# A diffusion block in float32 on one core: the later modulation sums go from VectorE to ScalarE and adding transfers

## The chip, the cores and the metric

The kernel runs on one core of a Trainium2 chip. The metric is the device time of one execution in microseconds (us). TensorE multiplies matrices, VectorE and ScalarE work element by element, GpSimd clears tiles and issues some transfers, SyncE issues the large ones. In the profile they are PE (with PEld for the loading of its weights), DVE, ACT, POOL and SP; a q behind the name (SPq) means the engine's instruction queue.

## What is computed

One layer of a diffusion backbone on 256 latent tokens and 256 context tokens of width 2048. Six modulation vectors come from the conditioning vector and one large matrix, `ada_w` (2048 x 12288):

```python
mod_lat = (silu_c @ ada_w[l] + ada_b[l])[:, None, :]
sh1, sc1, g1, sh2, sc2, g2 = jnp.split(mod_lat, 6, axis=-1)
h = modulate(rms_norm(x, norm1_w[l]), sh1, sc1)
f, q, k, v, z, gate = split_proj(h @ w_in[l])
att = neighborhood_attention(q, k, v, k_ctx, v_ctx, na_rpb[l])
x = x + g1 * gated_merge(f, att, z, gate, *mix_w)
h2 = modulate(rms_norm(x, norm2_w[l]), sh2, sc2)
x = x + g2 * conv_ffn(h2, *ffn_w)
return rms_norm(x, final_norm_w)
```

The shift and scale of the first norm (`sh1`, `sc1`) are needed at once. The other four vectors, `g1`, `sh2`, `sc2` and `g2`, are the later modulation: 4 x 2048 columns, in 16 blocks of 512 columns, each a sum over the 2048 channels.

## The kernel before

All weights stream from HBM in the order of their use. `chunk` (L84) cuts them from blocks of 3072 columns on 128 partitions (1.5 MB); SyncE loads each block with one transfer (L89) into one of three buffers `raw` (two more exist until the keys and values are done). A chunk is 1024 columns (512 KB), so a block holds three.

A chunk of ordinary weights is split for TensorE: ScalarE casts it to a high part `whi` (L98), VectorE subtracts to get the low part `wlo` (L99), and three products of the parts follow (L108 to L110). There are three buffers for such split chunks.

The later modulation runs beside this. A job is one block of 512 columns and takes eight chunks; the class `Side` (L188) traces one such piece after every few ordinary chunks, by a rate: 0.5 in the last groups of keys and values, 1 in the queries, 0.65 from the attention to the output projection, 0.2 in the gated MLP. So the chunks of later modulation lie between the others in the same blocks. `ada_sum` (L214) sums a piece: the channels lie on partitions, and VectorE multiplies each half chunk (512 columns) by a column of `sc` and adds it to an accumulator, in one instruction (L219). What is left is a sum over the partitions, by TensorE with ones: `ada_col` (L237) for `sh2` and `sc2`, with the accumulator `acc`, and `ada_row` (L223) for `g1` and `g2`, where the accumulator is the gate's own tile `g`, cleared by GpSimd and with its bias row loaded.

The order on each engine is set by a scheduler when the program is built, and each engine works through its own in order, waiting on semaphores. GpSimd's queue also holds the loads of small inputs and of the attention's biases (L428, two buffers). Stages in the profile: norm 1, keys and values to 252 us; queries to 300; attention, Fourier mixing and spatial gating, then gates and branch projections, to some 860; output projection and norm 2 to 985; the gated MLP after that.

Of the kernel before, what the change touches and what calls it, by code (L numbers as in the profile page):

```python
# [8 lines left out]
F32 = mybir.dt.float32  # L9
# [6 lines left out]
P = 128  # L16
# [38 lines left out]
def block_kernel(ctx: ExitStack, tc: tile.TileContext, a: dict):  # L55
    nc = tc.nc
    act, dve, pe = nc.scalar, nc.vector, nc.tensor

# [1 line left out]
    const = ctx.enter_context(tc.tile_pool(name="const", bufs=1))  # L60
    rawp = ctx.enter_context(tc.tile_pool(name="rawp", bufs=RAW_BUFS))
    spl = ctx.enter_context(tc.tile_pool(name="spl", bufs=3))
    tmp = ctx.enter_context(tc.tile_pool(name="tmp", bufs=T2K))
    small = ctx.enter_context(tc.tile_pool(name="small", bufs=4))
    pp = {}

    def psum_phase(name, **bufs):
        """banks of the accumulators, of the attention and of everything else"""
        if pp:
            pp["stack"].close()  # L70
        pp["stack"] = ExitStack()
        pp["pool"] = pp["stack"].enter_context(tc.tile_pool(name="ps_" + name, bufs=1, space=PSUM, reuse_waits="tile"))
        pp["bufs"] = bufs
# [6 lines left out]

    # the weights stream in, in the order of their use: blocks of RAWN columns, one transfer each
    stream = a["stream"]
# [28 lines left out]

# [1 line left out]
    ident = const.tile([P, P], F32, name="ident")  # L113
# [18 lines left out]

    # conditioning vectors: silu, split for the tensor engine, filled up to the columns of an array tile
    sc = const.tile([P, KT, 2], F32, name="sc")
    act.activation(sc, cc, AF.Silu)

# [1 line left out]
    rb_pool = ctx.enter_context(tc.tile_pool(name="rb", bufs=KT, side="left"))  # L138
    # the inputs wait where the low parts of the normed ones will be
    xs = [rb_pool.tile([P, 512], F32, name="xs", tag="rb") for _ in range(KT)]  # L140
# [3 lines left out]
    h_hi = ra_pool.tile([P, KT, 512], F32R, name="h_hi")  # L144
    # latent tokens in columns 0..255, context tokens and later the branch results in 256..511
    b_hi = h_hi[:, :, T:2 * T]
# [4 lines left out]

# [1 line left out]
    x_stack = ExitStack()  # L153
# [5 lines left out]
    act.copy(cs4[:, :, 0:2], sc)  # L159
    # brings in the table that the norm needs  # L160
    warm = small.tile([P, 1], F32, name="warm", tag="warm", bufs=1)
# [22 lines left out]

# [1 line left out]
    # sums over the contraction tiles on VectorE, a piece after every few chunks  # L186
    class Side:
        """Work that is traced piece by piece among the weights, `rate` pieces for each chunk of them."""  # L188

# [23 lines left out]

    def ada_sum(acc, blk):  # L214
        for c in range(8):
            w = chunk(1024, "ada_l", blk, c)
            for kk in range(2):
                k = c * 2 + kk
                dve.scalar_tensor_tensor(acc, w[:, kk * 512:(kk + 1) * 512], sc[:, k, 0:1], acc,  # L219
                                         op0=ALU.mult, op1=ALU.add)  # L220
            yield

    def ada_row(dst, blk, brow):  # L223
        """dst = the 512 columns of the block, on every partition."""
        acc = dst()
        nc.gpsimd.memset(acc, 0.0)
        nc.gpsimd.dma_start(acc[0:1], a["adab_rows"][brow])
        yield from ada_sum(acc, blk)
        hi, lo = split_w(acc, 512)
        o = psum("misc")  # L230
        pe.matmul(o, ones_r, hi[:, 0:512], start=True, stop=False)
        pe.matmul(o, ones_r, lo[:, 0:512], start=False, stop=True)
        act.copy(acc, o)
# [3 lines left out]
    def ada_col(which, blk, b):  # L237
        acc = tmp.tile([P, 512], F32, name="acc", tag="acc", bufs=2)
        nc.gpsimd.memset(acc, 0.0)
        yield from ada_sum(acc, blk)  # L240
        o = psum("misc")
        for j in range(4):
            pe.matmul(o[:, j:j + 1], acc[:, j * P:(j + 1) * P], ones[:, 0:1], start=True, stop=True)  # L243
        dst = mod2[:, which, 4 * b:4 * b + 4]
        dve.tensor_tensor(dst, o[:, 0:4], adab[:, 2 + which, 4 * b:4 * b + 4, 0], op=ALU.add)
        if which == 1:
            dve.scalar_tensor_tensor(dst, dst, 1.0, nw[:, 1, 4 * b:4 * b + 4, 0], op0=ALU.add, op1=ALU.mult)
# [8 lines left out]

# [1 line left out]
    def ada_part(k, c, pm):  # L258
        """products with the few conditioning rows, on four column tiles of the array side by side"""
        src = chunk(1024, "ada_e", k, c)  # L260
        for q in range(4):
            pe.matmul(pm[32 * q:32 * q + 32, 0:2 * P], cs4[:, 4 * c + q, :], src[:, 2 * q * P:2 * (q + 1) * P],  # L262
                      start=(c == 0), stop=(c == KT // 4 - 1))
# [21 lines left out]
    def kv_part(g, task, i, n):  # L285
        """a piece of a task: 512 columns of keys or values for n channels of group g"""
        k0, ng = KV_GROUPS[g]
# [44 lines left out]

    # the modulation of a group's channels is spread among the pieces of the group before, LEAD parts ahead
    for g, (k0, n) in enumerate(KV_GROUPS):
# [9 lines left out]

# [1 line left out]
    convs = load_const("convs", [P, FT, 4])  # L346
# [34 lines left out]
    def proj_a(key, nk, lhs, ntt, evac):  # L381
        """lhs(k, t): the split stationary operand of contraction tile k, token tile t; 512 columns of weights move."""
        outs = [psum() for _ in range(ntt)]
# [21 lines left out]

# [1 line left out]
    # branch results, transposed: f in 0..3, attention in 4..11, gMLP in 12..15  # L407
    # the queries of a head wait where its result will be
    for b in range(4):
# [51 lines left out]

# [1 line left out]
    f_sb = [None, None]  # L463
# [16 lines left out]

# [1 line left out]
    u = [None, None]  # L482
# [38 lines left out]

# [1 line left out]
    g1_stack = ExitStack()  # L523
# [7 lines left out]
    for nb in range(NB):  # L531
        gate = {}
        for br in range(3):
            def ev_g(t, o, br=br, nb=nb):
                gate[br, t] = t2k()
                act.activation(gate[br, t], o, AF.Sigmoid)
                if nb == NB - 1 and br == 2 and t == 1:
                    # brings in the table that the next norm needs
                    warm = small.tile([P, 1], F32, name="warm", tag="warm", bufs=1)
# [16 lines left out]

# [1 line left out]
    fp = ctx.enter_context(tc.tile_pool(name="fp", bufs=1, side="right", reuse_waits="tile"))  # L558
# [12 lines left out]
    def ev_o(t, o, c0, c1, part):  # L571
        cs = slice(c0, c1)
        # the gates of these columns are there
        assert len(later_mod.jobs) <= NB - 1 - c0 // 512, len(later_mod.jobs)
# [5 lines left out]
    for nb in range(NB - 1):  # L580
        proj_a(("wo", nb), KT, lhs_m, NT, lambda t, o, nb=nb: ev_o(t, o, nb * 512, (nb + 1) * 512, nb))
    # the last columns in two parts; of the second one token tile after the other
    woh = m_stack.enter_context(tc.tile_pool(name="woh", bufs=KT // 4, side="left", reuse_waits="tile"))
# [15 lines left out]

# [1 line left out]
    banks = [psum(tag) for tag in ("acc", "acc", "misc", "misc", "att", "att")]  # L601
# [36 lines left out]

# [1 line left out]
    g2p = ctx.enter_context(tc.tile_pool(name="g2p", bufs=1, side="left", reuse_waits="tile"))  # L640
# [43 lines left out]
    def down(c, hid):  # L684
# [35 lines left out]

        # the last columns one token tile after the other, so that the first one's end hides behind the second
        nb = NB - 1
# [41 lines left out]
def _host_layout(inp):  # L764
# [6 lines left out]
    def chan(w, n=KT):  # L771
        """[n*P] -> [P, n]"""
        return w.reshape(n, P).T

    def kblk(w):
        """[K*P, n] -> [P, K*n]"""
        K = w.shape[0] // P
# [20 lines left out]
    A["fnw"] = np.broadcast_to(g["final_norm_w"], (P, D))  # L798
    # transforms of the two Fourier axes (shapes alone)
    n = np.arange(T)  # L800
# [5 lines left out]
    A["dft_h"] = np.stack([np.cos(ah), -np.sin(ah)], axis=1) * float(P) ** -0.5  # L806
    # relative position bias laid out by query and key, the constant fill outside the window
    rpb = g["na_rpb"][0]
# [12 lines left out]
def _host_stream(inp, stream):  # L821
    """The weights in the order of their use: one contiguous run for each partition of each block."""
    import numpy as np
# [62 lines left out]
```

## Time and profile before

| | us |
|---|---|
| median of 2 runs | 1638.84 |
| the runs | 1638.11, 1639.57 |
| span of the profiled execution | 1640.9 |
| TensorE busy | 1605.3 |
| VectorE busy | 1096.6 |
| ScalarE busy | 742.0 |

The durations below come from the one profiled execution, whose span is 2.1 us above the median of the runs; the profile gives no other time for that execution. A busy share says how long an engine had an instruction in it. DMA share is the mean busy share of the core's 16 DMA engines. The clock granted to TensorE in a window stands as a fraction of full speed, and is 1.00 in all stages that matter here.

### The profile page before, as it was taken

How to read it: one execution, taken by the hardware profiler on the slowest of the kernel's cores; microseconds unless marked ns; L12 is line 12 of the kernel's file. 1: busy time of each engine (PE TensorE's matmuls, PEld its weight loads, DVE VectorE, ACT ScalarE, POOL GpSimd, SP SyncE). 2: the span in 40 equal slices, each digit the busy share in tenths (PEclk: the TensorE clock that was granted, in tenths of full speed). 3: DMA queues.
4: the chain of work that ended last, by engine and by line, in shares of the span. 5: the costliest groups of instructions: out<-in, count | busy, mean ns of one | idle time of the engine just before them, and what ended most of it. 6: DMA issues, size and time to landing. Idle time of an engine off the chain costs nothing.

```text
span 1640.9 us, 23497 instructions
## 1 busy us (share of the span) xinstructions
PE 1605.3 (98%) x9742; PEld 1383.1 (84%) x9742; DVE 1096.6 (67%) x1471; ACT 742.0 (45%) x986; POOL 28.5 (2%) x60
## 2 busy tenths in 40 slices
PE   5999999999999999999998999999999999999997
PEld 3667789878888888888888999899989998899896
DVE  4755668979987886544566666566666665555757
ACT  6423313557534444434454444444444444344344
POOL 1000001000100000000001000000000000000000
PEclk9999999999999999999999999999999999999999
DMA  9777747746687786544662565666665655454543
GB/s 380 304 308 291 285 149 289 299 170 247 224 318 290 290 305 267 187 181 178 237 226 113 208 224 212 220 225 229 231 222 216 221 227 184 180 183 186 192 180 129
DMA packets 38813, 377.80 MB, mean 230 GB/s; under 512 B 4945, under 2 KB 4961, under 8 KB 8881
## 3 DMA queue, kind: packets, MB, share of 16 engines
q1 hardware_dynamic: 36864, 369.66, 60.0%
q0 software_dynamic: 1840, 6.63, 1.1%
q8 instruction: 76, 1.25, 0.3%
q14 instruction: 33, 0.26, 0.1%
HBM read 374.17 MB, written 2.10 MB: 229 GB/s over the span
## 4 chain that ended last, share of the span: by engine, by line
PE 96%; DMA 2%; DVE 1%; ACT 1%; SPq 0%; issue 0%; ACTq 0%; DVEq 0%
PE ps_acc L108 30%; PE ps_acc L110 30%; PE ps_acc L109 30%; PE ps_misc L262 2%; DMA raw<-in_w 1%; PE ps_att L108 0%; PE ps_misc L271 0%; PE ps_att L109 0%; PE ps_att L110 0%; DMA xs<-in_xct 0%; PE ps_att L445 0%; PE ps_misc L243 0%; DVE t2k L610 0%; SPq L166 0%; DVE wlo L99 0%; PE ps_misc L552 0%
## 5 line engine op out<-in xcount | busy, mean ns | idle before, releaser
L99 DVE TENSOR_TENSOR wlo<-raw,whi 128x1024 fp32r<-128x1024 f32 (+1 forms) x504 | 606.6, 1206 | 358.9 <-ACT whi L98 355.8
L98 ACT CAST whi<-raw 128x1024 fp32r<-128x1024 f32 (+1 forms) x504 | 519.9, 1034 | 597.6 <-PE ps_acc L110 367.0
L109 PE MATMUL ps_acc<-h_lo,whi 128*128 128x256 f32 (+1 forms) x1664 | 482.4, 290 | 0.0
L108 PE MATMUL ps_acc<-h_lo,whi 128*128 128x256 f32 x1408 | 396.2, 281 | 3.7 <-ACT hm L622 3.7
L110 PE MATMUL ps_acc<-h_lo,wlo 128*128 128x256 f32 x1408 | 395.9, 281 | 0.0
L109 PEld LDWEIGHTS ps_acc<-h_lo,whi 128*128 128x128 f32 x1664 | 314.8, 189 | 5.0
L108 PE MATMUL ps_acc<-whi,h_hi 128*128 128x512 f32 x736 | 293.0, 401 | 0.0
L110 PE MATMUL ps_acc<-whi,h_lo 128*128 128x512 f32 x736 | 292.7, 398 | 0.0
L109 PE MATMUL ps_acc<-wlo,h_hi 128*128 128x512 f32 x736 | 290.3, 394 | 0.0
L108 PEld LDWEIGHTS ps_acc<-h_lo,whi 128*128 128x128 f32 x1408 | 266.7, 189 | 4.2 <-ACT hm L622 3.9
L110 PEld LDWEIGHTS ps_acc<-h_lo,wlo 128*128 128x128 f32 x1408 | 266.8, 189 | 0.0
L108 PEld LDWEIGHTS ps_acc<-whi,h_hi 128*128 128x128 f32 x736 | 138.0, 188 | 36.5 <-issue 5.0
L109 PEld LDWEIGHTS ps_acc<-wlo,h_hi 128*128 128x128 f32 x736 | 139.0, 189 | 33.0 <-issue 0.5
L110 PEld LDWEIGHTS ps_acc<-whi,h_lo 128*128 128x128 f32 x736 | 137.8, 187 | 33.6 <-issue 0.5
L108 PE MATMUL ps_acc<-whi,hid_hi 128*128 128x512 f32 (+1 forms) x358 | 140.8, 393 | 0.0
L110 PE MATMUL ps_acc<-whi,hid_lo 128*128 128x512 f32 (+1 forms) x358 | 140.1, 391 | 0.0
L109 PE MATMUL ps_acc<-wlo,hid_hi 128*128 128x512 f32 (+1 forms) x358 | 139.2, 389 | 0.0
L219 DVE SCALAR_TENSOR_TENSOR g<-raw,sc,g 128x512 f32<-128x512 f32 x128 | 95.7, 748 | 26.0 <-DMA raw<-in_w 24.8
L219 DVE SCALAR_TENSOR_TENSOR acc<-raw,sc,acc 128x512 f32<-128x512 f32 x128 | 95.6, 747 | 7.9 <-DMA raw<-in_w 6.3
L108 PE MATMUL ps_acc<-h_hi,whi 128*128 128x512 f32 (+1 forms) x256 | 88.0, 344 | 0.7 <-DVE v L310 0.7
L110 PE MATMUL ps_acc<-h_hi,wlo 128*128 128x512 f32 (+1 forms) x256 | 85.6, 338 | 0.0
L110 PEld LDWEIGHTS ps_acc<-whi,hid_lo 128*128 128x128 f32 x358 | 67.2, 188 | 16.4
(186 smaller groups left out, 1359.5 us busy)
## 6 DMA issues: line engine op xcount, KB each, us to landing
raw<-in_w SPq DMA_DIRECT2D x231, 1536.0 KB, 6.5
xs<-in_xct SPq DMA_DIRECT2D x16, 256.0 KB, 5.6
bias<-in_bias POOLq DMA_DIRECT2D x16, 128.0 KB, 3.8
x<-in_x_tok POOLq DMA_DIRECT2D x1, 2048.0 KB, 8.7
out_dram<-x SPq DMA_DIRECT2D x8, 256.0 KB, 3.1
raw<-in_fnw POOLq DMA_DIRECT2D x1, 1024.0 KB, 5.3
dft_n<-in_dft_n POOLq DMA_DIRECT2D x1, 512.0 KB, 3.8
gnw<-in_gnw POOLq DMA_DIRECT2D x1, 256.0 KB, 4.2
```

Of the source, the lines that this page charges most:

```text
L98: act.copy(hi, src)
L99: dve.tensor_tensor(lo, src, hi.bitcast(F32), op=ALU.subtract)
L108: pe.matmul(out, l_hi, r_hi, start=start, stop=False)
L109: pe.matmul(out, l_hi, r_lo, start=False, stop=False)
L110: pe.matmul(out, l_lo, r_hi, start=False, stop=stop)
L219: dve.scalar_tensor_tensor(acc, w[:, kk * 512:(kk + 1) * 512], sc[:, k, 0:1], acc, op0=ALU.mult, op1=ALU.add)
L262: pe.matmul(pm[32 * q:32 * q + 32, 0:2 * P], cs4[:, 4 * c + q, :], src[:, 2 * q * P:2 * (q + 1) * P], start=(c == 0), stop=(c == KT // 4 - 1))
```

## The change

`ada_sum` no longer uses VectorE for the products. ScalarE multiplies each half chunk by its column, the first chunk of a block into a new tile `part` (1024 columns, two buffers), the seven others in place in the raw buffer. For those seven GpSimd issues a transfer from the raw buffer to `part` that adds as it writes. After the last, VectorE adds the two halves of `part`; `ada_row` adds the result to the gate's tile, `ada_col` uses `part` instead of `acc`, whose clears are gone. The room that GpSimd's transfers have for descriptors is set to 8192.

```diff
+    adap = ctx.enter_context(tc.tile_pool(name="adap", bufs=1))
...
-    def ada_sum(acc, blk):
+    def ada_sum(part, blk):
+
         for c in range(8):
             w = chunk(1024, "ada_l", blk, c)
             for kk in range(2):
-                k = c * 2 + kk
-                dve.scalar_tensor_tensor(acc, w[:, kk * 512:(kk + 1) * 512], sc[:, k, 0:1], acc,
-                                         op0=ALU.mult, op1=ALU.add)
+                ks = slice(kk * 512, (kk + 1) * 512)
+                act.activation((w if c else part)[:, ks], w[:, ks], AF.Copy, scale=sc[:, 2 * c + kk, 0:1])
+            if c:
+                nc.gpsimd.dma_start(part, w, accum_op=ALU.add)
             yield
+        dve.tensor_tensor(part[:, 0:512], part[:, 0:512], part[:, 512:1024], op=ALU.add)
+
+    def ada_part_of():
+        return adap.tile([P, 1024], F32, name="part", tag="part", bufs=2)
...
         acc = dst()
         nc.gpsimd.memset(acc, 0.0)
         nc.gpsimd.dma_start(acc[0:1], a["adab_rows"][brow])
-        yield from ada_sum(acc, blk)
+        part = ada_part_of()
+        yield from ada_sum(part, blk)
+        dve.tensor_tensor(acc, acc, part[:, 0:512], op=ALU.add)
...
-        acc = tmp.tile([P, 512], F32, name="acc", tag="acc", bufs=2)
-        nc.gpsimd.memset(acc, 0.0)
+        acc = ada_part_of()
         yield from ada_sum(acc, blk)
...
-    nc = _bacc.Bacc("TRN2", target_bir_lowering=False, num_devices=1)
+    nc = _bacc.Bacc("TRN2", target_bir_lowering=False, num_devices=1, dynamic_dma_scratch_size=8192)
```

The rest of the diff takes comments out. Lines of the changed kernel lie up to nine further down: L219 becomes L221 (the multiplication) and L223 (the transfer), L98 and L99 become L99 and L100, L89 becomes L90.

The order on the engines, at three places. ScalarE in the first gates and branch projections (window 430 to 640 us of the profile before), a piece of the order before; `raw` with a number is one block of weights, `whi` the high part of a chunk, L536 the gate's activation:

```order
L98 CAST whi_3991<-raw_3989 128x1024
L98 CAST whi_4007<-raw_3989 128x1024
L98 CAST whi_4042<-raw_4040 128x1024
L98 CAST whi_4058<-raw_4040 128x1024
L536 ACTIVATE t2k_4034<-ps_acc_3877 128x512
L536 ACTIVATE t2k_4036<-ps_acc_3878 128x512
L98 CAST whi_4078<-raw_4076 128x1024
L98 CAST whi_4096<-raw_4076 128x1024
```

and about the same place now (the numbers of the tiles are counted anew, L544 is the former L536):

```order
L221 ACTIVATE raw_3942<-raw_3942,sc_92 128x512
L544 ACT_TABLE_LOAD
L544 ACTIVATE t2k_3876<-ps_acc_3713 128x512
L544 ACTIVATE t2k_3878<-ps_acc_3714 128x512
L99 CAST whi_3926<-raw_3901 128x1024
L221 ACTIVATE raw_3967<-raw_3967,sc_92 128x512
L99 CAST whi_3944<-raw_3942 128x1024
L221 ACTIVATE raw_3967<-raw_3967,sc_92 128x512
L99 CAST whi_3963<-raw_3942 128x1024
```

Between the casts stand multiplications in place, some of a block that is loaded after the one cast next; each has to wait for its block's landing, and the casts behind it wait with it. In the order before, such instructions stood on VectorE.

GpSimd in the attention, before, with what each waits for (names with DMASW are landings of its own transfers, with DMAHW those of SyncE's loads):

```order
L428 DMA bias_2544<-in_bias 128x256 [waits DMAHW4_49,DMAHW3_49,DMAHW6_49,DMAHW1_49,DMASW1_49]
L428 DMA bias_2585<-in_bias 128x256 [waits DMASW2_49]
L239 MEMSET acc_2336 128x512 [waits PE_49]
L239 MEMSET acc_2781 128x512 [waits DVE_49,PE_49]
L428 DMA bias_2647<-in_bias 128x256 [waits DMASW3_49,DMASW1_49,DVE_49]
L428 DMA bias_2688<-in_bias 128x256 [waits DMASW4_49,DMASW2_49,DVE_49]
L239 MEMSET acc_3433 128x512 [waits PE_49]
L428 DMA bias_2750<-in_bias 128x256 [waits DMASW5_49,DMASW3_49,DVE_49]
L428 DMA bias_2801<-in_bias 128x256 [waits DMASW6_49,DMASW4_49,DVE_49]
```

and now:

```order
L223 DMA part_2360<-raw_2391 128x1024 [waits DMASW1_49,DMASW0_49,Activation_49]
L223 DMA part_2360<-raw_2457 128x1024 [waits DMASW2_49,DMAHW0_49,DMASW1_49,Activation_49]
L223 DMA part_2360<-raw_2494 128x1024 [waits DMAHW1_49,DMASW2_49,Activation_49]
L223 DMA part_2360<-raw_2494 128x1024 [waits DMASW3_49,Activation_49]
L223 DMA part_2360<-raw_2560 128x1024 [waits DMAHW2_49,DMASW4_49,Activation_49]
L436 DMA bias_2676<-in_bias 128x256 [waits DVE_49]
L223 DMA part_2360<-raw_2664 128x1024 [waits DMASW7_49,DMAHW3_49,DMASW5_49,Activation_49]
L436 DMA bias_2717<-in_bias 128x256 [waits DVE_49]
L223 DMA part_2812<-raw_2879 128x1024 [waits DMAHW5_49,PE_49,Activation_49]
L436 DMA bias_2780<-in_bias 128x256 [waits DMASW6_49,DVE_49]
```

The loads of the biases now stand between adding transfers, and each of these waits for ScalarE and for the landing of the transfer before it or, with a new `part`, for what used that tile last.

SyncE's loads in the first gates, before:

```order
L89 DMA raw_3919<-in_w 128x3072 [waits DMAHW3_49,DVE_49,Activation_49]
L89 DMA raw_3955<-in_w 128x3072 [waits DMAHW4_49,DVE_49,Activation_49]
L89 DMA raw_3989<-in_w 128x3072 [waits DMAHW5_49,DVE_49]
L89 DMA raw_4040<-in_w 128x3072 [waits DMAHW6_49,DVE_49]
L89 DMA raw_4076<-in_w 128x3072 [waits DMAHW7_49,DVE_49]
```

and now:

```order
L90 DMA raw_3901<-in_w 128x3072 [waits DMAHW1_49,DMASW2_49,DVE_49]
L90 DMA raw_3942<-in_w 128x3072 [waits DMAHW2_49,DMASW3_49,DVE_49]
L90 DMA raw_3967<-in_w 128x3072 [waits DMAHW3_49,DMASW7_49,DVE_49]
L90 DMA raw_4004<-in_w 128x3072 [waits DMAHW4_49,DMASW1_49,DVE_49]
L90 DMA raw_4040<-in_w 128x3072 [waits DMAHW5_49,DMASW2_49,DVE_49]
L90 DMA raw_4091<-in_w 128x3072 [waits DMAHW6_49,DMASW3_49,DVE_49]
```

A load now also waits for one of GpSimd's transfers (DMASW), the one that read the buffer's block last.

## Rows read from the trace of the kernel before

**Rows 1.** The page: busy times of the engines, and the chain by engine.

```profile
PE 1605.3 (98%) x9742; PEld 1383.1 (84%) x9742; DVE 1096.6 (67%) x1471; ACT 742.0 (45%) x986; POOL 28.5 (2%) x60
...
PE 96%; DMA 2%; DVE 1%; ACT 1%; SPq 0%; issue 0%; ACTq 0%; DVEq 0%
```

**Rows 2.** Windows: PE, PEld, DVE, ACT, POOL busy (instructions), clock, DMA share, GB/s.

```profile
24.00:92.00 68.00, 66.77 (x435) 44.76 (x427) 42.84 (x81) 30.26 (x54) 0.00 (x0) 1.00 0.84 335
92.00:202.00 110.00, 109.93 (x674) 78.50 (x669) 67.18 (x116) 35.19 (x57) 0.00 (x0) 1.00 0.78 298
...
252.00:300.00 48.00, 47.34 (x398) 46.91 (x397) 40.39 (x52) 18.45 (x22) 1.06 (x2) 1.00 0.81 314
300.00:430.00 130.00, 128.63 (x642) 103.70 (x641) 114.60 (x220) 83.19 (x132) 12.52 (x24) 1.00 0.59 217
430.00:640.00 210.00, 210.00 (x927) 169.97 (x926) 172.86 (x205) 91.81 (x102) 0.49 (x1) 1.00 0.79 300
...
985.00:1600.00 615.00, 615.00 (x4310) 572.75 (x4310) 381.83 (x454) 278.02 (x340) 0.56 (x1) 1.00 0.56 207
```

**Rows 3.** Windows of line L219 alone: VectorE busy (instructions), then as before.

```profile
92.00:202.00 110.00, 14.95 (x20) 1.00 0.78 298
...
252.00:300.00 48.00, 17.97 (x24) 1.00 0.81 314
300.00:430.00 130.00, 27.66 (x38) 1.00 0.59 217
430.00:640.00 210.00, 69.30 (x93) 1.00 0.79 300
...
985.00:1330.00 345.00, 37.43 (x50) 1.00 0.61 224
```

**Rows 4.** Waits of SyncE and of GpSimd: us in total, times, longest.

```profile
SPq L89 <- DVE wlo L99: 1021.8, 157, 33.0
...
POOL bias L428 <- DVE ps_att L431: 99.2, 12, 18.0
```

**Rows 5.** Waits of ScalarE, 430 to 640 us.

```profile
ACT whi L98 <- PE ps_acc L110: 97.8, 61, 2.2
```

**Rows 6.** Timeline of ScalarE, 541 to 549 us: start, duration, instruction, idle before.

```profile
544.47 1.05 ACT L98 CAST whi<-raw 128x1024 fp32r<-128x1024 f32 x1 [1.75 <-PE ps_acc L110]
547.27 1.05 ACT L98 CAST whi<-raw 128x1024 fp32r<-128x1024 f32 x1 [1.75 <-PE ps_acc L110]
```

**Rows 7.** The page: DMA issues, count, KB each, median us to landing.

```profile
raw<-in_w SPq DMA_DIRECT2D x231, 1536.0 KB, 6.5
...
x<-in_x_tok POOLq DMA_DIRECT2D x1, 2048.0 KB, 8.7
...
raw<-in_fnw POOLq DMA_DIRECT2D x1, 1024.0 KB, 5.3
dft_n<-in_dft_n POOLq DMA_DIRECT2D x1, 512.0 KB, 3.8
```

**Rows 8.** Lines by shape: count, busy us, mean ns of one, idle before.

```profile
L219 DVE SCALAR_TENSOR_TENSOR g<-raw,sc,g 128x512 f32<-128x512 f32 x128 | 95.7, 748 | 26.0 <-DMA raw<-in_w 24.8
L219 DVE SCALAR_TENSOR_TENSOR acc<-raw,sc,acc 128x512 f32<-128x512 f32 x128 | 95.6, 747 | 7.9 <-DMA raw<-in_w 6.3
...
L547 DVE TENSOR_TENSOR t2k<-t2k 128x512 f32<-128x512 f32 x16 | 10.4, 683 | 0.0
...
L745 ACT ACTIVATE x<-x,rstd 128x512 f32<-128x512 f32 x4 | 2.7, 711 | 0.2 <-DVE rstd L568 0.2
```

**Rows 9.** DMA issues in 302 to 303 us, and in 319.9 to 320.1 us.

```profile
bias<-in_bias POOLq DMA_DIRECT2D x1, 128.0 KB, 7.0
...
bias<-in_bias POOLq DMA_DIRECT2D x1, 128.0 KB, 2.3
```

## The prediction

> **What bounds the kernel now.** I read the page's busy times and its chain first. TensorE is busy 98% of the 1640.9 us span and holds 96% of the chain that ended last [rows 1]. The idle rest is 1640.9 - 1605.3 = 35.6 us, most of it before the first weights. So whatever is taken off VectorE, no more than 35.6 us can come back, and the sum below looks for what is added.
>
> Second, the windows by stage [rows 2]. The reader is to see that TensorE is full in all of them, while the share of the DMA engines is not: 0.78 at 92 to 202 us, 0.81 at 252 to 300 (queries), 0.59 at 300 to 430 (attention), 0.79 at 430 to 640 (the rest of gating, first gates), 0.56 in the gated MLP. The same window view for the line of the sums alone [rows 3] tells why: the stages with a high share are those in which the modulation weights come in beside the others. A piece is two instructions, so there are 10, 12, 19 and 46.5 pieces in these four stages and 25 in 985 to 1330.
>
> Third, the waits. SyncE stood 1021.8 us in front of its next load until VectorE's last split freed a buffer [rows 4]; with three buffers of 1.5 MB each load starts when one is released, and no sooner. ScalarE waits on TensorE for its split buffers (97.8 us in 430 to 640) [rows 5], so splits run up to three chunks ahead; a chunk is 2.8 us of TensorE, the distance between casts [rows 6]. The lead is thus at most 3 x 2.8 = 8.4 us, and a load takes 6.5 us from issue to landing [rows 7]. Any further delay of a release soon reaches TensorE.
>
> **The change part by part.**
>
> *VectorE.* Removed: 256 instructions of 0.748 us, 95.7 + 95.6 = 191.3 us [rows 8]. Added: 16 joins of halves and 8 sums for the rows, 24 x 0.683 us by an addition of the same shape (L547) = 16.4 us [rows 8]. Net -175 us, beside a TensorE that hardly waits for VectorE: gain 0 to 35.6 us by the idle above; I take 0, since the largest idle parts lie at the start and at the tail, where there is no sum.
>
> *ScalarE.* Added: 256 multiplications. The nearest row is L745, a scaled copy in place by a column of scales, 0.711 us [rows 8]: 182 us in all. By stage: 430 to 640, 91.8 + 93 x 0.711 = 158 of 210 us; 252 to 300, 18.5 + 24 x 0.711 = 35.5 of 48; 300 to 430, 83.2 + 38 x 0.711 = 110 of 130 [rows 2, 3]. There is room in each and the wait on TensorE [rows 5] hides it: 0. If the cover is gone, the cast behind a multiplication is late by the wait of that multiplication for its block, which VectorE's sums had before too (the order of ScalarE in the change section).
>
> *GpSimd's transfers.* Added: 16 blocks x 7 = 112 transfers of 512 KB, in the five stages 7/8 of the pieces: 8.75, 10.5, 16.6, 40.7 and 21.9. Each waits for the multiplication and for the landing of the one before on the same tile, and SyncE's next load waits for it (the orders of GpSimd and SyncE): a release that ended with VectorE now ends with a landing. No row shows an adding transfer. By landing, the nearest rows of the same queue are 512 KB in 3.8 us, 1024 KB in 5.3 us and 2048 KB in 8.7 us [rows 7]; the first is the transfer if adding costs nothing, the last if it takes four times the data. By engine time: 300 GB/s at a share of 0.79 is 380 GB/s when all 16 are busy [rows 2], so 524,288 bytes take 1.38 us per pass. An adding transfer must read the weights and the sum and write the sum: two reads, 1 MB. I take two passes, 2.76 us, the row of 1024 KB; the ends are less than one pass and four passes.
>
> The Trainium skill has a rule on this ("Collectives: The Full Stack", section "The bandwidth ceiling: the fold count and why AG ≠ RS ≠ AR"): an add in the DMA path is slow not by the addition but since it reads two sources, which halves the rate. By that rule it is two passes; no run here shows it yet.
>
> *The sum* is demand against time, in us of the 16 engines:
> - 252 to 300: 0.81 x 48 = 38.9, plus 10.5 x 2.76 = 29.0, is 67.9 in 48.
> - 430 to 640: 0.79 x 210 = 165.9, plus 40.7 x 2.76 = 112.3, is 278.2 in 210.
> - 300 to 430: 0.59 x 130 = 76.7, plus 16.6 x 2.76 = 45.8, is 122.5 in 130.
> - 92 to 202: 0.78 x 110 = 85.8, plus 24.2, is 110.0 in 110; there are five buffers here, I take 0.
> - 985 to 1330: 0.61 x 345 = 210, plus 60, is 270 in 345; a piece comes every 13.8 us, longer than even 8.7 us: 0.
>
> Full use is not to be had with three buffers: the highest share of a stage in this trace is 0.84, at 24 to 92 [rows 2]. Between 0.84 and 1 I take 0.92. Then 67.9 / 0.92 = 73.8 (+25.8), 278.2 / 0.92 = 302.4 (+92.4), 122.5 / 0.92 = 133.2 (+3.2): +121 us. At a share of 1 it is 19.9 + 68.2 = +88; at 0.84, 32.8 + 121.2 + 15.8 = +170. The span becomes 1640.9 + 121 = 1762, and the median of the runs lies 2.1 us below the span: **1760 us**, between 1727 and 1809 for this case alone.
>
> *The rest.* Eight clears on GpSimd go, and an engine busy 2% [rows 1] gains nothing for the path. The smaller descriptor scratch I price at 0; were it too small, GpSimd's issues would grow longer.
>
> **Rivals.**
>
> *One pass (0.22).* Adding costs no more than a copy: 53.4 / 0.92 = 58.0 (+10.0) and 222.1 / 0.92 = 241.4 (+31.4), with nothing at 300 to 430: +41, 1680 us; 1656 at a share of 1, 1709 at 0.84. For it: the 512 KB row is as quick as the others. Against it: the sum must be read as well.
>
> *Not slower (0.10).* The transfers fit into the gaps of the queue. The place is 430 to 640, where the engines stand idle 210 - 165.9 = 44 us; it decides where one transfer takes under 44 / 40.7 = 1.08 us of the engines (252 to 300: 9.1 / 10.5 = 0.87 us), or where loads slide into the emptier 300 to 430. Then VectorE's freed time releases other blocks sooner and the time is 1637 to 1640 us, with a small chance of a few us more gained. Against it: one plain pass is 1.38 us, and three buffers let little slide.
>
> By the Trainium skill ("DMA: Bandwidth & Descriptors", section "Anatomy of one DMA — SWDGE (gpsimd) path") a transfer from GpSimd takes 2 us and its bytes at 436 GB/s, an estimate of 3.2 us for 512 KB; seven in a chain are 22.4 us, less than the 36 us that eight pieces have in 430 to 640, so by it alone the chain keeps up and this rival holds. The trace agrees only where the queue is empty: of two 128 KB transfers one landed in 2.3 us, and one beside loads in 7.0 us [rows 9].
>
> *Three or four passes (0.15).* Adding is slower than its bytes. Four passes, 5.52 us each: (38.9 + 58.0) / 0.92 = 105 (+57), (165.9 + 224.7) / 0.92 = 425 (+215), (76.7 + 91.6) / 0.92 = 183 (+53), and 92 to 202 (85.8 + 48.3) / 0.92 = 146 (+36): +361, some 2000 us. Three passes: +41, +153, +28 and +23, +245, 1884 us. For it: nothing in the trace; against it: nothing either.
>
> *GpSimd's queue (0.08).* The biases of the attention stand in it 99.2 us for their buffers, 12 waits, the longest 18.0 us [rows 4], and now additions stand behind them, with raw buffers held. Only what exceeds the lead of 8.4 us counts: for the longest 9.6 us, for some four waits at most 40 us on top of one pass, 1720 us. It would show as TensorE idle at 300 to 430 and not at 430 to 640.
>
> **How the numbers follow.** Two passes has 0.45. The range runs from 1660 to 1890: it holds two passes, nearly all of one pass, the queue, and three passes; left out are the unchanged time, the lower end of one pass and four passes, some 0.2. A measurement of this kernel can tell about 2%, 33 us: slower starts at 1672. Below it lie the hidden case (0.10, of which 0.02 may be a gain over 2%) and the lower third of one pass (0.07): faster 0.02, same 0.15, slower 0.83.
>
> **What would show it.** Right: TensorE idle at what are now 252 to 300 and 430 to 640, ended by ScalarE or VectorE, and these ended by loads of the raw blocks; SyncE waiting for GpSimd's transfers; a DMA share near 0.9 there; the gated MLP unchanged; an adding transfer that lands in 5 us or more. Wrong: a share that stays near 0.8 while transfers land late (the chain, not the engines, is the limit), idle time in the attention alone (the queue), or ScalarE full with loads landed.

## The result, and the profile after

The changed kernel takes **1935.3 us** (median of 2 runs, 1930.36 to 1940.23) against 1638.84 before: a ratio of 1.181, 95% interval 1.173 to 1.188, so 296 us slower. The forecast was 1760 us, with a range from 1660 to 1890. The profiled execution is the one of 1940.23 us, so the sums below come to 298 us.

First the page of the changed kernel: the engines' busy times, and the groups and issues of what was added (columns as in [rows 1, 7, 8]).

```profile
PE 1668.6 (86%) x9742; PEld 1419.7 (73%) x9742; DVE 939.7 (48%) x1239; ACT 894.3 (46%) x1242; POOL 123.1 (6%) x164
...
L221 ACT ACTIVATE raw<-raw,sc 128x512 f32<-128x512 f32 x224 | 151.9, 716 | 189.0 <-DMA raw<-in_w 188.8
...
L225 DVE TENSOR_TENSOR part<-part 128x512 f32<-128x512 f32 x16 | 11.1, 692 | 172.4 <-DMA part<-raw 172.4
...
raw<-in_w SPq DMA_DIRECT2D x231, 1536.0 KB, 7.0
part<-raw POOLq DMA_DIRECT2D x112, 512.0 KB, 9.5
```

TensorE is no longer full. Its idle time rose from 35.6 us to 1938.5 - 1668.6 = 269.9 us, and its busy time by 63.3 us for the same 9742 matmuls. VectorE and ScalarE are both under half busy, so neither is short of time. The two groups of the new sums each lost time to a transfer: ScalarE's multiplications 188.8 us to loads of weights, VectorE's joins 172.4 us to the adding transfers, which land in 9.5 us.

Where the time went, by stage. For each bound of [rows 2], the first matmul that starts behind it in the trace of before was looked up by its number in TensorE's order in the trace of after; the column is what its start lost within the stage.

| stage of before, us | 0–202 | 202–252 | 252–300 | 300–430 | 430–640 | 640–860 | rest | all |
|---|---|---|---|---|---|---|---|---|
| forecast | 0 | 0 | +25.8 | +3.2 | +92.4 | 0 | 0 | +121 |
| after | +4.5 | +12.7 | +23.8 | +78.3 | +182.3 | +0.1 | -4 | +298 |

By the same matmuls, the stages 252 to 300, 300 to 430 and 430 to 640 of before are 269 to 341, 341.2 to 549.4 and 549.4 to 941.7 us of after. The windows of after (columns as in [rows 2]); the second starts where the loss does, and the last is a part of the gated MLP:

```profile
92.00:202.00 110.00, 108.02 (x666) 76.45 (x666) 52.47 (x96) 44.78 (x72) 6.11 (x7) 1.00 0.90 314
202.00:252.00 50.00, 43.01 (x186) 34.74 (x184) 14.25 (x22) 21.17 (x30) 7.25 (x10) 0.94 0.76 214
...
341.20:549.40 208.20, 148.24 (x641) 115.67 (x640) 99.14 (x190) 110.09 (x179) 29.72 (x42) 0.85 0.76 204
549.40:941.70 392.30, 248.54 (x926) 191.09 (x925) 113.13 (x118) 142.74 (x189) 34.91 (x40) 0.79 0.80 212
1281.00:1896.00 615.00, 615.00 (x4325) 573.07 (x4324) 352.65 (x410) 307.93 (x390) 19.71 (x23) 1.00 0.66 227
```

The reader is to see the DMA share. In the two stages that lost 261 of the 298 us it is 0.76 and 0.80. That is up from 0.59 in the first, and in the second no more than the 0.79 at which TensorE was full before; [rows 2] has up to 0.84. Fewer GB/s are moved than the 217 and 300 of before. The DMA engines had time left in both. The gated MLP is full as before.

The waits of after: engine, line, what ended the wait, us in total, times, longest.

```profile
SPq L90 <- DVE wlo L100: 834.8, 127, 32.1
SPq L90 <- DMA part<-raw: 632.5, 76, 15.3
...
ACT raw L221 <- DMA raw<-in_w: 188.8, 42, 12.9
DVE part L225 <- DMA part<-raw: 172.4, 16, 22.9
...
POOL bias L436 <- DVE ps_att L439: 39.3, 7, 11.3
...
PE ps_misc L251 <- DVE part L225: 48.1, 3, 20.7
...
PE ps_att L453 <- DVE e L446: 45.1, 7, 11.3
PE ps_acc L110 <- DVE wlo L100: 42.0, 15, 18.0
PE ps_acc L109 <- ACT whi L99: 42.0, 12, 6.9
...
PE ps_misc L240 <- ACT whi L99: 29.6, 2, 16.9
```

TensorE's own waits, the last five lines, tell by which ways the delay reaches it. 42.0 + 42.0 us end with the splits of an ordinary chunk, which come late when its block does. 48.1 + 29.6 us end with what stands behind the join of a block (L251 is the product of `ada_col`, L240 that of `ada_row`, which waits for the sum's cast). 45.1 us end with a step of the attention on VectorE (L446).

A second row stands beside one of before. SyncE waited 1021.8 us for VectorE's splits [rows 4]; now it waits 834.8 us for them and 632.5 us for adding transfers. The same wait within 341.2 to 941.7 us, and the transfers issued and landed there:

```profile
SPq L90 <- DMA part<-raw: 502.1, 51, 15.3
```

```profile
raw<-in_w SPq DMA_DIRECT2D x58, 1536.0 KB, 8.4
part<-raw POOLq DMA_DIRECT2D x60, 512.0 KB, 9.7
```

For 502 of 600.5 us SyncE stood before a load whose buffer an adding transfer was the last to release. And the transfers run in a row: taken one by one from the trace, at least one of the 60 is under way in 511 of the 600.5 us (85%), and 52 of them start within 1.3 us of the landing of the one before. In 35 of these ScalarE's last multiplication had ended over 0.7 us before the start, so there it was the landing that was waited for, although the brackets below name instructions of ScalarE. How a step of it goes is seen in SyncE's and GpSimd's timelines, in a window with three such steps (start, duration, instruction, idle before); first SyncE, in 506 to 507, 516.4 to 517.4 and 526.8 to 527.6 us:

```profile
506.14 0.33 SPq L90 DMA_DIRECT2D raw<-in_w  x1
...
516.42 0.33 SPq L90 DMA_DIRECT2D raw<-in_w  x1
...
526.91 0.33 SPq L90 DMA_DIRECT2D raw<-in_w  x1
```

and GpSimd:

```profile
506.63 0.88 POOL L223 DMA_DIRECT2D part<-raw  x1 [9.38 <-ACT raw L221]
...
517.28 0.86 POOL L223 DMA_DIRECT2D part<-raw  x1 [9.19 <-ACT e L444]
...
527.29 0.86 POOL L223 DMA_DIRECT2D part<-raw  x1 [8.38 <-ACT h_hi L99]
```

The load of 506.14 landed after 8.4 us, at 514.6; the transfer of 506.63 after 9.7 us, at 516.37. At 516.42 the next load starts, into the buffer that this transfer had read; at 517.28 the next transfer, which adds to the same tile. One load and one transfer go off together, slow each other, and the next pair waits for the later landing: 10.3 to 10.5 us for each step, in **lockstep**.

### The profile page after: what moved, and what is told of

Its sections match the earlier page's. It is cut to its first block, busy times and chain, and to the rows that moved or that the text cites. A ratio compares the mean times of both kernels' runs of the same rounds, so it can differ in the third digit from the quotient of the medians.

```text
span 1938.5 us, 23824 instructions
## 1 busy us (share of the span) xinstructions
PE 1668.6 (86%) x9742; PEld 1419.7 (73%) x9742; DVE 939.7 (48%) x1239; ACT 894.3 (46%) x1242; POOL 123.1 (6%) x164
## 4 chain that ended last, share of the span: by engine, by line
PE 50%; DVE 1%; DMA 1%; issue 0%; ACT 0%; ACTq 0%; DVEq 0%; POOLq 0%
PE ps_acc L109 17%; PE ps_acc L111 17%; PE ps_acc L110 17%; DMA part<-raw 1%; DVE t2k L618 0%; PE ps_misc L560 0%; DVE hm L628 0%; DVE wlo L100 0%; ACT h_lo L99 0%; PE ps_misc L240 0%; PE ps_misc L241 0%; ACT hm L630 0%; DVE x L702 0%; DVE h_lo L100 0%; DVE t2k L701 0%
## 5 line engine op out<-in xcount | busy, mean ns | idle before, releaser
L100 DVE TENSOR_TENSOR wlo<-raw,whi 128x1024 fp32r<-128x1024 f32 (+1 forms) x504 | 605.9, 1207 | 605.5 <-ACT whi L99 604.0
L99 ACT CAST whi<-raw 128x1024 fp32r<-128x1024 f32 (+1 forms) x504 | 517.5, 1032 | 503.0 <-PE ps_acc L111 289.1
L109 PE MATMUL ps_acc<-whi,h_hi 128*128 128x512 f32 x736 | 309.8, 423 | 53.0 <-ACT whi L99 42.0
L110 PE MATMUL ps_acc<-wlo,h_hi 128*128 128x512 f32 x736 | 307.2, 417 | 42.0 <-DVE wlo L100 42.0
L111 PE MATMUL ps_acc<-whi,h_lo 128*128 128x512 f32 x736 | 305.8, 415 | 0.0
L221 ACT ACTIVATE raw<-raw,sc 128x512 f32<-128x512 f32 x224 | 151.9, 716 | 189.0 <-DMA raw<-in_w 188.8
L109 PEld LDWEIGHTS ps_acc<-whi,h_hi 128*128 128x128 f32 x736 | 147.3, 201 | 98.0 <-ACT whi L99 47.9
L110 PEld LDWEIGHTS ps_acc<-wlo,h_hi 128*128 128x128 f32 x736 | 148.6, 202 | 83.3 <-DVE wlo L100 48.1
L223 POOL DMA_DIRECT2D part<-raw x112 | 97.9, 887 | 1204.4 <-ACT raw L221 825.2
L111 PEld LDWEIGHTS ps_acc<-whi,h_lo 128*128 128x128 f32 x736 | 147.4, 200 | 35.8 <-issue 0.7
L225 DVE TENSOR_TENSOR part<-part 128x512 f32<-128x512 f32 x16 | 11.1, 692 | 172.4 <-DMA part<-raw 172.4
```

The source lines that it names most:

```text
L99: act.copy(hi, src)
L100: dve.tensor_tensor(lo, src, hi.bitcast(F32), op=ALU.subtract)
L109: pe.matmul(out, l_hi, r_hi, start=start, stop=False)
L110: pe.matmul(out, l_hi, r_lo, start=False, stop=False)
L111: pe.matmul(out, l_lo, r_hi, start=False, stop=stop)
L221: act.activation((w if c else part)[:, ks], w[:, ks], AF.Copy, scale=sc[:, 2 * c + kk, 0:1])
```

## The experiments

Two theories were set against each other. *Engines*: the 16 DMA engines have too much to carry, as the forecast had it. *Chain*: each adding transfer waits for the landing of the one before (on `part`), and holds its raw buffer until it lands, so that the next load waits too; what counts is landings one behind the other, whatever the share. Each experiment is a single run beside one of the kernel before on the same chip, which took 1639.8 to 1640.8 us; the two runs of the changed kernel lie 10 us apart, so a smaller difference is not read as one.

### e1: VectorE adds the products, no transfers

```diff
-                nc.gpsimd.dma_start(part, w, accum_op=ALU.add)
+                dve.tensor_tensor(part, part, w, op=ALU.add)
```

> ScalarE multiplies as in the change, but VectorE adds the products (112 additions of 1024 columns) in place of the adding transfers. Theory transfers (the time goes into the transfers, by their landing and what waits for it): 1630 to 1660 us, as before the change. Rival ScalarE (its multiplications, placed in front of casts that TensorE needs, cost the time): over 1750 us, with TensorE idle at 300 to 640 us.

Measured: 1642.87 us, before 1640.8. The page:

```profile
L221 ACT ACTIVATE raw<-raw,sc 128x512 f32<-128x512 f32 x224 | 151.2, 716 | 20.0 <-DMA raw<-in_w 20.0
...
L223 DVE TENSOR_TENSOR part<-part,raw 128x1024 f32<-128x1024 f32 x112 | 136.8, 1222 | 16.4 <-ACT raw L221 15.2
...
raw<-in_w SPq DMA_DIRECT2D x231, 1536.0 KB, 6.3
```

ScalarE does the same 224 multiplications in the same 716 ns each, and waits 20.0 us for loads in place of 188.8. The time is the one expected if the transfers are the cause: multiplying in place on ScalarE costs nothing, and the transfers, with what waits for them, are the whole loss.

### e2: the transfers copy and do not add

```diff
-                nc.gpsimd.dma_start(part, w, accum_op=ALU.add)
+                nc.gpsimd.dma_start(part, w)
```

The sum over the chunks is left out; order, waits and sizes stay.

> The transfers copy in place of adding (the sum over a block's chunks is left out). A 4 KB packet should take 159 ns as the plain ones of before do, against 328 ns. Theory engine time (the 16 DMA engines' time alone is the bound): the excess of 297 us falls to the one-pass sum, +41 us, 1680 us. Theory chain (each transfer waits for the landing of the one before, 9.7 us beside a load): landings fall by some 2 us only, 1750 to 1820 us.

Measured: 1822.98 us, 112 less than with adding and still 182 over before. That is 143 us over what the engines' time alone would give, and just above the range of the chain. By stage: 0, +2.7, +23.4, +35.8, +116.4 and +1.6. Its windows of the attention and of the first gates, and then its issues in both:

```profile
326.10:491.90 165.80, 141.56 (x641) 111.42 (x640) 98.69 (x190) 108.95 (x178) 22.15 (x42) 0.92 0.71 250
491.90:818.30 326.40, 236.95 (x926) 185.41 (x925) 113.30 (x118) 142.95 (x189) 21.17 (x40) 0.84 0.75 255
```

```profile
raw<-in_w SPq DMA_DIRECT2D x57, 1536.0 KB, 7.6
part<-raw POOLq DMA_DIRECT2D x60, 512.0 KB, 8.0
```

This tells most. With the bytes of one pass the engines have a share of 0.71 and 0.75 (before: 0.59 and 0.79), far from full, and yet 152 us are lost in these two stages. One of the 60 transfers is under way in 399 of their 492.2 us (81%), and 50 of them start within 1.3 us of the landing before: a row again. The passes set how late a landing is, the row sets the time.

### e3: the joins three pieces later

```diff
+            if c == JOIN_AT:
+                ends_now()
...
-        dve.tensor_tensor(part[:, 0:512], part[:, 0:512], part[:, 512:1024], op=ALU.add)
...
+        def end():
+            dve.tensor_tensor(part[:, 0:512], part[:, 0:512], part[:, 512:1024], op=ALU.add)
...
+        ends.append(end)
```

> The join of a block's halves and what follows it stands three pieces later, in the middle of the next block. Theory joins (VectorE and TensorE stand in order behind a join that waits for the last landing, 172 us on VectorE, 48 on TensorE): 1780 to 1850 us. Theory chain: the transfers follow each other at the same distance of some 10 us, 1900 to 1940 us.

Measured: 1927.18 us. The waits of the joins, and of TensorE's products:

```profile
DVE part L263 <- DMA part<-raw: 92.4, 8, 16.8
PE ps_acc L111 <- DVE wlo L101: 78.8, 20, 15.5
DVE part L247 <- DMA part<-raw: 71.1, 8, 18.5
...
PE ps_acc L110 <- ACT whi L100: 50.4, 14, 6.3
```

VectorE still waits 92.4 + 71.1 = 163.5 us at the joins, against 172.4: the scheduler left them at their place in VectorE's order, to within one instruction. So of the edit that was meant only half was made, and the price of VectorE's waits stays open. TensorE's products behind the joins did move later. Their waits, 48.1 + 29.6 us in after, are 1.5 us here, and yet the time is 8 us less, no more than two runs differ. TensorE waits for splits instead, 78.8 + 50.4 us in place of 42.0 + 42.0. So what TensorE waits for behind the joins is no price of its own: while the transfers keep their pace, the same delay comes to it by the loads.

### e4: the attention's biases from SyncE's queue

```diff
-            nc.gpsimd.dma_start(bias, a["bias"][h_, t])
+            nc.sync.dma_start(bias, a["bias"][h_, t])
```

> The attention's biases are loaded from SyncE's queue in place of GpSimd's. Theory queue (biases behind adding transfers, and these behind biases, cost the 78 us at 300 to 430 us of before): 1855 to 1895 us. Theory chain: within 20 us of 1935 us.

Measured: 1935.72 us, the time of after, as the chain had it. GpSimd's queue is not the cause; in after the biases stood in it only 39.3 us.

### f1, f2, f3: the two links of the lockstep, each alone

f1 is after with a descriptor room of 4096, the control for the other two. f2 keeps the chain and lifts the hold: the products go to a tile of their own, so that the raw buffer is free once ScalarE has read it.

```diff
+            prod = adap.tile([P, 1024], F32, name="prod", tag="prod", bufs=2) if c else None
...
-                act.activation((w if c else part)[:, ks], w[:, ks], AF.Copy, scale=sc[:, 2 * c + kk, 0:1])
+                act.activation((prod if c else part)[:, ks], w[:, ks], AF.Copy, scale=sc[:, 2 * c + kk, 0:1])
...
-                nc.gpsimd.dma_start(part, w, accum_op=ALU.add)
+                nc.gpsimd.dma_start(part, prod, accum_op=ALU.add)
```

f3 keeps the hold and cuts the chain: even and odd chunks go to two tiles, each with its own first product, so that two transfers can be under way (6 per block in place of 7, 96 in all).

```diff
+        parts = [part, adap.tile([P, 1024], F32, name="part_b", tag="part_b", bufs=2)]
...
+                act.activation((w if c > 1 else parts[c])[:, ks], w[:, ks], AF.Copy, scale=sc[:, 2 * c + kk, 0:1])
+            if c > 1:
+                nc.gpsimd.dma_start(parts[c % 2], w, accum_op=ALU.add)
...
+        dve.tensor_tensor(part, part, parts[1], op=ALU.add)
```

> The changed kernel with 4096 in place of 8192 for GpSimd's descriptors: the control for the next two, which need the memory. If that room is not what makes transfers wait: 1925 to 1945 us. If it is: over 1960 us, with issues on GpSimd longer than 0.87 us.

> ScalarE writes the products into a tile of their own (two buffers), and the transfers add from there, so that a raw buffer is free after the multiplication. Theory hold (the loads wait for landings, 632 us on SyncE's queue, and start together with the next transfer): that wait is gone, 1700 to 1800 us. Theory chain (each transfer waits for the landing of the one before): the distance of the transfers stays at 9 to 10 us, now with ScalarE waiting for a product tile, 1880 to 1950 us.

> Odd and even chunks of a block add into two tiles that VectorE joins (96 transfers in place of 112, two of them may be under way at once). Theory chain: the distance halves where it was the limit, 1700 to 1800 us. Theory hold: the loads still wait for landings, 1860 to 1930 us, a seventh fewer transfers.

Measured: f1 1939.06, as expected, f2 1862.38 (-77 against f1), f3 1774.10 (-165). f2 missed both its ranges, 1700 to 1800 and 1880 to 1950; f3 is in that of the chain. The waits of f2, first SyncE's, then of the other engines, and its transfers in the two stages:

```profile
SPq L90 <- DVE wlo L100: 1222.8, 166, 32.6
```

```profile
ACT prod L222 <- DMA part<-prod: 135.4, 32, 10.0
DVE part L226 <- DMA part<-prod: 110.2, 16, 12.9
...
part<-prod POOLq DMA_DIRECT2D x60, 512.0 KB, 6.5
```

SyncE's wait for transfers is gone, as meant, and the chain now holds ScalarE at the product tiles. f2's 60 transfers land sooner, after 6.5 us in the median, but the row stays: one is under way in 424 of its 525.7 us of these two stages (81%), and 47 start within 1.3 us of a landing. So the 77 us are what lifting the hold gives with the chain in place. Then f3's windows of the two stages, and SyncE's waits:

```profile
324.70:481.40 156.70, 140.47 (x642) 110.57 (x640) 102.07 (x193) 109.43 (x178) 24.88 (x37) 0.91 0.79 243
481.40:774.30 292.90, 238.39 (x928) 184.16 (x926) 120.37 (x124) 143.80 (x190) 30.48 (x35) 0.89 0.93 279
```

```profile
SPq L90 <- DMA part<-raw: 207.9, 33, 12.1
SPq L90 <- DMA part_b<-raw: 184.4, 34, 14.7
```

With two chains the first gates reach a share of 0.93 and lose 82.9 us: here, for the first time, the engines are near full, at the share that the forecast had taken for all. The transfers of the two tiles overlap (50 by 9.2 us in the mean, under way in 327 of 449.6 us). 6 transfers in place of 7 take off a seventh of them; the loss fell by more than half. Both links are part of the cause, the chain the more.

### g1, g2, g3: the later modulation spread thinner

```diff
-RATE_1 = 1.0
-RATE_2 = 0.65
+RATE_1 = 0.4
+RATE_2 = 0.45
```

g1 is after with these rates (they set how many pieces are traced beside the ordinary chunks), g2 is f3 with them, g3 is the kernel before with them, the control.

> The changed kernel with rates of 0.4 in the queries and 0.45 from the attention on, in place of 1 and 0.65, so that a piece comes every 6.2 us of TensorE's work and not every 4.3, and the sums reach further into the stage of before at 640 to 985 us. Theory chain: a transfer every 7 to 10 us is still later than its piece, but the transfers run beside more of TensorE's work: 1700 to 1780 us. Rival fixed price (each transfer takes some 4.5 us from TensorE wherever it lies, 260 us over 57 transfers): 1900 us and more.

> The thinner rates with two chains of transfers for each block (96 transfers in place of 112, 4096 for the descriptors). Theory chain: with twice the time for each transfer they are done before their buffers are wanted, 1640 to 1690 us. Rival engine time (two passes of each transfer beside the loads): not far from one chain, 1700 us or more.

> The kernel before with the thinner rates, as the control of these: 1635 to 1650 us, since TensorE is full at either rate.

Measured: g1 1873.3 us, g2 1741.13, g3 1643.52; g3 is as expected. Both theories missed in g1: the chain had it at 1700 to 1780 us, its rival over 1900. By stage g1 lost +30.2 at 300 to 430, +108.2 at 430 to 640 and +92.3 at 640 to 860, where the pieces now also lie. SyncE's wait in g1 at 462.9 to 1093.5 us, the last two of these stages together, and the issues there:

```profile
SPq L90 <- DMA part<-raw: 407.7, 49, 11.5
```

```profile
raw<-in_w SPq DMA_DIRECT2D x72, 1536.0 KB, 8.4
part<-raw POOLq DMA_DIRECT2D x54, 512.0 KB, 9.7
```

A transfer is under way in 489 of the 630.6 us (78% for 85%), so the row is a little more open. But 49 of the 72 loads still start on a landing, most transfers still go off together with a load, and both still land as late as in after. My expectation had counted the gaps between the transfers and not this hold. g2 missed its 1640 to 1690 too: it is 33 us better than f3 and 98 us over g3, and its loads wait 249 of 498.3 us for landings at these stages. Its rival of engine time had said 1700 us or more; with a DMA share of 0.86 there, this run does not exclude it.

### h1, h2: thin rates with an own tile, and late joins

h1 joins g1's rates and f2's edit; h2 adds e3's edit, six pieces late.

> The thinner rates and the products in a tile of their own (one chain, 4096 for the descriptors). Theory hold (with the thin rates a load and a transfer still start together, since the load waits for the landing that frees its buffer): most of the 233 us that the thin rates left goes, 1690 to 1760 us, and landings near 5 us. Rival chain alone (the transfers of a block in a row are the limit at any rate): above 1820 us.

> As the one before, and the join of a block six pieces later, when its last transfer has long landed. Theory joins (VectorE stands in order behind a join, and TensorE waits for the low parts behind it): the wait at the joins, 172 us with the thin rates, falls under 30 us and the time by 40 to 100 us more, to 1640 to 1690 us. Rival (the joins stand beside waits that are there anyway): within 15 us of the kernel before it.

Measured: h1 1793.62 us, 80 less than g1. It lies between the 1690 to 1760 that was expected if the hold were the rest of it and the 1820 of its rival, so both missed; its transfers land in 6.8 us in the median where near 5 was expected. h2 1798.25; the joins' wait in it is

```profile
DVE part L264 <- DMA part<-prod: 59.7, 8, 11.4
DVE part L248 <- DMA part<-prod: 54.7, 8, 11.6
```

114.4 us, against 117.3 in h1. Again the scheduler did not let the joins move on VectorE, and the run says nothing on their price.

**What the table of runs says.** Against f1 the own tile gives 77 us, the thin rates (g1) 66, both (h1) 145, about the sum: hold and density add up here. Two chains give 165 and with the thin rates (g2) 198, where the sum would be 231: those overlap. No version beats the kernel before, and none of this kind can by much: it has 35.6 us of idle on TensorE, and its sums on VectorE cost it nothing (e1, g3).

## Why the prediction was wrong

**Right.** ScalarE at 0 and VectorE at 0 (e1: +2 us in all, with 137 us of adding still on VectorE). The gated MLP at 0: a transfer lands in 5.9 us there between 1281 and 1640, with a piece every 14 us. The queries: +23.8 for +25.8, though e2 lost as much there (+23.4) with half the engine time, so that the number was met by a sum that does not hold. GpSimd's queue at nothing (e4) and the descriptor room at nothing: with 4096 in place of 8192 (f1) the time lies between the two of after, and GpSimd's issues take 887 ns in the mean in both.

**Two passes were right too.** By the packets' records, one of 4 KB takes 328 ns in the median where it adds and 159 ns where it only copies (e2). A transfer is 128 of them, eight for each of the 16 engines: 2.62 us, for the 2.76 that the sum took, and 1.27 for the 1.38 of one pass. The Trainium skill's rule ("Collectives: The Full Stack", section "The bandwidth ceiling: the fold count and why AG ≠ RS ≠ AR"), that an add reads two sources and so runs at half the rate, agrees with this: 328 / 159 = 2.06.

**The step that failed** is the sum itself: "Between 0.84 and 1 I take 0.92", the division of the demand by a share, as though the engines would always have something to carry. At 300 to 430 and 430 to 640 the share was 0.76 and 0.80, and the losses +78.3 and +182.3 in place of +3.2 and +92.4. By its own terms: engine time came out as 0.80 x 392.3 = 314 us where the sum had 278.2, and 0.76 x 208.2 = 158 for 122.5. At a share of 0.92 these would have been 341 and 172 us, losses of 131 and 42. So of the 165 us missed in the two stages some 39 + 39 are engine time that the sum lacked (packets that lie beside adds take longer: a raw packet of 12 KB 642 ns in the mean in 350 to 800 us, 519 in before), and 51 + 36 are the share. The 0.84 that it was taken from belongs to a stage with five buffers (24 to 92 us) and said nothing of three. And that share is no quantity of the engines here: e2 halves the demand of the transfers and it falls to 0.71 and 0.75, f3 lets two of them run at once and it rises to 0.93 in the first gates.

What stands in its place is the lockstep. An adding transfer lands in 4.5 us alone and in 9.6 to 9.7 us beside a load. Issues of after at three times, 699.5 (no load under way), 689.3 and 763.8 us:

```profile
part<-raw POOLq DMA_DIRECT2D x1, 512.0 KB, 4.5
...
raw<-in_w SPq DMA_DIRECT2D x1, 1536.0 KB, 8.2
part<-raw POOLq DMA_DIRECT2D x1, 512.0 KB, 9.6
...
raw<-in_w SPq DMA_DIRECT2D x1, 1536.0 KB, 8.2
part<-raw POOLq DMA_DIRECT2D x1, 512.0 KB, 9.7
```

The forecast had the chain in view: it says that a release "now ends with a landing", but no term of its sum prices that, and it put the chain into the wrong rival: with the Trainium skill's 3.2 us for a transfer it kept up, and so it stood for "not slower". Two rows already said otherwise: 2.3 us alone and 7.0 us beside loads for 128 KB [rows 9]. With that factor of 3 on the 3.8 us of a 512 KB copy [rows 7] a transfer would have been some 11 us, seven of them 80 us for each block where eight pieces had 36 us; measured, seven by 9.7 are 68. That rival, a row of landings, was missing on the slow side, though the forecast names its sign: a share that stays near 0.8 while transfers land late. The rule behind the 3.2 us ("DMA: Bandwidth & Descriptors" of the Trainium skill, section "Anatomy of one DMA — SWDGE (gpsimd) path", 2 us and the bytes at 436 GB/s) holds for neither landing of an adding transfer here, 4.5 or 9.7 us; the copies of e2 that had nothing beside them took 2.9 us in the median, near it.

**92 to 252, forecast 0, was +17.** At 92 to 202 the sum had seen 110 us of demand in 110 and I had put it at nothing: the share is 0.90 there, and 4 us are lost. Most, 12.7 us, is lost at 202 to 252, for which the sum had no term, and there the share is only 0.76. e2 lost 2.7 us in it and f3 6.2, while g1, with the adding but the thinner rates that follow, lost nothing at a share of 0.85. So this is not the engines' time; that it is the same row of landings is likely and not shown.

**TensorE's clock was no term at all.** It was granted 1.00 in these stages before and 0.85 and 0.79 after, means over stretches at 1.00 and at 0.50 (2.4 and 1.2 GHz), where TensorE had idled between its matmuls; their busy time rose by 148.24 - 128.63 = 19.6 and 248.54 - 210.00 = 38.5 us, 58 of the 63.3. How much of that the time pays is open: where TensorE waits for loads anyway, slower matmuls need not cost anything, and no run kept the clock up beside late transfers.

**Still open:** what is left if chain and hold are lifted together (own tiles and two chains), which was not tried; the price of VectorE's waits at the joins, since both runs on them left these where they were.

## What to carry to other kernels

A transfer that adds into a tile is a link of a chain: count its landing, as it is beside the traffic of that stage, times the links in a row, and hold that against the time that the pieces have; the mean share of the DMA engines does not show it. Ask also whose buffer it holds until it lands, since a load that waits for it starts together with the next transfer and both land late. And work that lies free on an engine beside a full TensorE is not worth moving to a resource that feeds TensorE.

## What was not expected of the hardware

- An adding packet takes twice the time of a copying one (328 and 159 ns for 4 KB), and GpSimd's issue is longer too: 871 to 887 ns in the mean for one that adds, 530 ns in e2.
- A landing of 512 KB doubles beside one load of 1.5 MB (4.5 to 9.7 us), and the load goes from 6.5 us [rows 7] to 8.4. The transfer, a third as large, lands after the load. Both are 128 packets; why they end so near each other is not shown.
- Half of the engine time in the transfers (e2) lowered the DMA share and won 112 us: the share fell while the kernel became faster.
